# A decoder block's gate/up stage: accumulator X read as a whole, T4 ahead of B22 in the first pair, a ninth place for raw weights, other sums reloaded

## The chip, the cores and the metric

The kernel runs on one core of a Trainium2 chip. The metric is the device time of one execution in microseconds, as the median over several runs. The profile is one execution on the same core; its engines are called PE (TensorE, matmul), DVE (VectorE), ACT (ScalarE), POOL (GpSimd) and SP (SyncE, which here issues most of the DMAs).

## The reference, cut to what matters

The block takes 1024 rows of 1024 numbers in float32. It computes a combined input projection, a causal pooling mixer and a differential attention, merges the two by gates, projects the result, and then runs a feed-forward block. The change touches the feed-forward block alone:

```python
u = rms_norm(h, ffn_pre_g)                                    # (1024, 1024)
f = jax.nn.silu(u @ w_ffn_gate) * (u @ w_ffn_up)              # (1024, 2816)
h = h + rms_norm(f @ w_ffn_down, ffn_post_g)
```

All of it is in float32.

## The kernel before, in words

**Precision.** A float32 product is made of three matmuls in the type fp32r. Each operand is split into a rounded part `hi` (a copy on ACT) and the remainder `lo` (a subtraction on DVE), and `triple` (L2024) adds hi·hi, hi·lo and lo·hi into one accumulator in PSUM.

**Seven products in place of eight.** `u` transposed is cut into four blocks: halves of the contraction by halves of the rows. The weights are cut the same way: halves of the contraction by gate and up. A product of two such 2x2 block matrices is computed with seven block products (Winograd's form of Strassen's method). With g0, g1 the two contraction halves of a block of 128 gate columns and u0, u1 those of the up columns, the weight operands are B11 = g0, B21 = g1, T1 = u0 - g0, T2 = u1 - T1, T3 = u1 - u0, T4 = g1 - T2 and B22 = u1. Their partners are A11, A12, S1, S2, S3, A22 and S4, sums of blocks of `u`. Products are numbered 1 (B11), 2 (B21), 3 (B22), 4 (T4), 5 (T1), 6 (T2) and 7 (T3). Three accumulators take them up:

- Y receives products 1, 6, 7 and 4 in turn. Between two of them its value is copied out by ACT, as the starts of the four results "11", "12", "22" and "21". After product 4, ACT takes the gate's silu straight from Y.
- X receives product 5 and, on top of it, product 3. After product 5 DVE adds X to "22" (in a place named p5); after product 3 it adds X to "12" (in u2).
- Z receives product 2, which DVE adds to "11".

The gated hidden block is silu("11") times "12" for one half of the rows and silu("21") times "22" for the other.

**Units and pairs.** There are 22 blocks of 128 hidden columns. Two blocks, kb and kb + 11, make a group. Group 0 is done ahead of this stage, group 1 as two single units (`unit_products`), and groups 2 to 10 as nine *pairs* (`pair`, L1792). In a pair, each product is done for both blocks, first half "a", then half "b": `P5a` is product 5 of the first block. One such half is 12 matmuls of 128x128 by 128x512. For a pair, X is one tile of two banks, `[128, 2, 512]`, one bank for each block; Y and Z are two tiles each.

**A second level.** From pair 2 on, product 2 of both blocks together is itself done by seven smaller products; from pair 3 on also product 3, and from pair 4 on product 4. Step `3.6` is the sixth inner product of product 3: six matmuls of 128x128 by 128x256 into accumulators Yi, Zi or Xi, each read by an addition on DVE. The sums of blocks that serve as inner operands are formed once on DVE, ahead of their first pair. They don't all fit on chip, and those that the table `STREAM` names are stored to DRAM (`isd`) and loaded again in every pair.

**What sets the order.** The stage isn't written in the order in which it runs. `pair_products` (L1596) states PE's order from the table `STEADY` and hands each operation to a planner (`Plan`), with what it reads and writes, a cost and a due time; a helper's line stands in the profile for all of a kind (L1428 additions and subtractions on DVE, L1432 copies on ACT, L1443 activations, L1446 DMAs). The planner simulates the engines, gives each operation a place (a slot of a pool) when it starts, and emits everything in order of its planned starts. From that order the framework makes the waits between engines, from the tiles that each instruction reads and writes. Raw weights, sums before their split and hidden blocks live in the pool "vf" (eight places of 128x1024 float32, two of which hold the first hidden block and are named F), split operands in the pool "vr" (sixteen).

For PSUM tiles the planner orders a tile's readers and writers on different engines; for a tile of kind "banks" it does so for each bank by itself. In `STEADY`, half `P5a` and half `P5b` of product 5 stand next to each other in pair 2, where `3.x` and `4.x` drop out, and have the steps 3.7, 3.3 and 4.1 between them in later pairs.

The lines that the change touches:

Of the kernel before, what the change touches and what calls it, by code (L numbers as in the profile page):

```python
# [16 lines left out]
P = 128  # L17
# [22 lines left out]

CAPS = {"vr": 16, "vf": 8, "mm": 2, "fil": 2, "pair": 2, "b4": B4, "a8": A8, "wraw": 2, "whi": 2, "wlo": 2, "ft": 2, "sg": 2,
        "small": 20}
BANKS = ("mm", "fil", "pair")
RESERVE = {"E": 2, "gate": 2, "row": 2, "uw": 2}
# [1334 lines left out]

HIDDEN_PATIENCE = {"DVE": 0.05, "ACT": 0.05}
FIRST = {"2": 2, "4": 4, "3": 3}
STREAM = ("2S2", "2S3", "2S4", "3S3", "3S4", "4S2", "4S3")
STASHED, STASH_STEP = range(3, 11), 22
SHARED = ()
OPERANDS = {"2": ("B21", "A12"), "3": ("B22", "S4"), "4": ("T4", "A22")}
# [13 lines left out]
def paired(pl, k, U):  # L1401
# [194 lines left out]
    def pair_products(W, I, T, deep, order, tail, done_with, gated=None):  # L1596


        Y = [bank("mm", "Y") for _ in range(2)]
        X = bank("pair", "X", "banks")  # L1600
        Z = [bank("fil", "Z") for _ in range(2)] if "2" not in deep else None
        acc = {"Y": [(y, None, y) for y in Y], "X": [(X, e, lambda e=e: X()[:, e, :]) for e in range(2)]}
        if Z:
            acc["Z"] = [(z, None, z) for z in Z]
        steps, done = {}, set()
        needs = [{"P1", "P6", "P5", "3.4" if "3" in deep else "P3", "2.4" if "2" in deep else "P2"},
                 {"P7", "P5", "4.4" if "4" in deep else "P4"}]

        def outer(n, e):
            o, w, a = OUTER[n]  # L1610
            s, key, v = acc[o][e]
            product(s, key, v, W[w][e], a, n in "152")
            at = clock[0]

            def to(x):
                t, kt = T[x][e]
                copy(t, v, HALF, [(s, key)], [kt], at + .5)

            def add(x):
                t, kt = T[x][e]  # L1620
                tt(t, v, t, ALU.add, HALF, [(s, key), kt], [kt], at + 2)

            if n == "1":
                to("11")
            if n == "6":
                to("12")
            if n == "7":
                to("22")
                if "4" in deep:
                    to("21")  # L1630
            if n == "5":
                add("22")
                if "3" in deep:
                    add("12")
            if n == "3":
                add("12")
            if n == "2":
                add("11")
            if n == "4":
                gated(e, v, (s, key), at)  # L1640

        def one(x):
            if x[0] == "P":
                outer(x[1], "ab".index(x[2]))
                if x[2] == "b":
                    done.add(x[:2])
            else:
                if x[0] not in steps:
                    steps[x[0]] = inner_steps(W[OPERANDS[x[0]][0]], I[x[0]], T[{"2": "11", "3": "12", "4": "21"}[x[0]]])
                steps[x[0]](x[2])  # L1650
                done.add(x)
            for i in range(2):
                if needs[i] and needs[i] <= done:
                    needs[i] = None
                    done_with(i, clock[0])

        late = {}
        for x in order:
            if x[-1] == "'":
                if x[:-1] in tail:  # L1660
                    tail.pop(x[:-1])()
            elif x[0] != "P" and x[0] not in deep or x[0] == "P" and x[1] in deep:
                continue
            else:
                one(x)
        for x in [x for x in tail]:
            tail.pop(x)()
        if "4" in deep and "4.4" not in order:
            late = {x: (lambda x=x: one(x)) for x in ("4.6", "4.2", "4.7", "4.3", "4.4")}
        return late  # L1670
# [4 lines left out]
def hidden(pl, k):  # L1675
# [116 lines left out]
    def pair(kb, tail):  # L1792
        deep = [x for x in "234" if kb >= FIRST[x]]

        def load(i, kh):
            w = ("w_ffn_gate", "w_ffn_up")[i]
            s = v4(F32, 2, 4, P)
            for e in range(2):
                f = kb + e * FP
                dma(lambda e=e: s()[:, e], lambda f=f: getattr(k, w)[kh * HALF:(kh + 1) * HALF, f * P:(f + 1) * P].rearrange(  # L1800
                    "(k p) n -> p k n", p=P), .26, w=[(s, f"{h + 1}{e + 1}") for h in range(2)])
            return s

        def stashed():
            s = v4(F32, 2, 4, P)
            for e in range(2):
                j, h = divmod(kb - STASHED[0], 2)
                dma(lambda e=e: s()[:, e], lambda e=e: k.tsd[j][:, e, :, h * P:(h + 1) * P], .26,
                    w=[(s, f"{h + 1}{e + 1}") for h in range(2)])
            return s  # L1810

        W = t.pair_weights(load, deep, stashed if kb in STASHED else None)
        q = new_hidden()
        up, p5 = ([temp(s) for _ in range(2)] for s in ("u2", "p5"))
        T = {"11": [q["11"], q["12"]], "21": [q["21"], q["22"]], "12": [(x, x) for x in up], "22": [(x, x) for x in p5]}
        both = set()

        def finish(i, at):
            for e in range(2):
                v, key = q[f"{i + 1}{e + 1}"]  # L1820
                u = (up, p5)[i][e]
                if i == 0 or "4" in deep:
                    silu(v, v, [key], [key], at + 2 + e)
                tt(v, v, u, ALU.mult, HALF, [key, u], [key], at + 3 + e)
            both.add(i)
            if len(both) == 2:
                keep_hidden(kb, q)

        def gated(e, v, key, at):
            o, ko = q[f"2{e + 1}"]  # L1830
            silu(o, v, [key], [ko], at + 1)

        I = {x: t.fetched(x, I2[x]) for x in deep}
        return t.pair_products(W, I, T, deep, STEADY, tail, finish, gated)

    def first_operands():

# [48 lines left out]
def block_kernel(ctx, tc, x, w_in, pool_mix, pool_scale, w_branch_a, lam_q1, lam_k1, lam_q2,  # L1886
# [71 lines left out]
    make_identity(nc, ident)  # L1958
    mhalf = cp.tile([P, 8], F32, name="mhalf")
    nc.vector.memset(mhalf, -0.5)  # L1960
    junk = cp.tile([P, D], mybir.dt.bfloat16, name="junk")
    psc = cp.tile([P, 4], F32, name="psc")
    sgc = cp.tile([P, 1], F32, name="sgc")
    cnt = cp.tile([P, 4, 16], F32, name="cnt")
# [319 lines left out]
    def place(pool, i):  # L2284
        if (pool, i) not in cells:
            if pool == "vr":
                if i < 8:
                    v = W[("B11", "T1", "T2", "B22")[i // 2]][i % 2]().rearrange("p a k n -> p (a k n)")
                else:
                    v = b4([P, D], F32R, "v") if i < B4 else wp.tile([P, D], F32R, tag="wlo", bufs=2, name=name("v"))  # L2290
            elif i < 2:
                v = F[:, i].rearrange("p t c -> p (t c)")
            elif i < 4:
                both = a8([P, 2, D], F32, "v")
                cells["vf", 2], cells["vf", 3] = both[:, 0], both[:, 1]
                v = cells[pool, i]
            else:
                v = wp.tile([P, D], F32, tag=("wraw", "whi", "wlo")[(i - 4) // 2], bufs=2, name=name("v"))
            cells[pool, i] = v
        return cells[pool, i]  # L2300

# [216 lines left out]
```

## Time and profile before

| what | value |
|---|---|
| median of 3 runs | 1237.06 us (1237.05 to 1237.63) |
| the profiled execution's own time | 1236.96 us |
| its span, from the first to the last instruction | 1235.2 us |
| PE busy | 1224.2 us (99% of the span) |
| DVE busy | 965.5 us (78%) |
| ACT busy | 615.1 us (50%) |
| granted TensorE clock, mean | 0.999 |
| gate/up stage | about 647 to 1021 us |

Times in a row of the timeline are the start in us from the span's start, then the duration in us. Behind an instruction the tile it writes stands left of "<-", what it reads to the right; buffer numbers are left out, so that `p` is a place p1 or p5, `u` is u2, and `v`, `Wh`, `Wl`, `F` are places of the pools under the names that they had when they were made. A bracket gives the idle time of the engine just before, and who ended it. Matmuls overlap: one that is recorded as 0.39 us long is followed by the next after less than that, so that the step from start to start is the measure of PE's pace. A row of the table of waits gives the total, the number and the longest of them.

### The profile page before, as it was taken

The page shows a single profiled execution, that of the slowest core. Times are in us where ns is not written, and L with a number is a line of the kernel's source. Part 1 is how long each engine was busy: PE and PEld are TensorE (multiplying, and loading weights), DVE is VectorE, ACT ScalarE, POOL GpSimd, SP SyncE. Part 2 cuts the span into 40 slices and gives each one's busy share as a digit, 9 for nine tenths or more (in the row PEclk, how much of TensorE's full clock was granted, in tenths as well). Part 3 has the DMA queues.
Part 4 walks back from the last instruction along what each step waited for, and adds up shares of the span by engine and source line. Part 5 has one row for each costly group of instructions (what it writes and reads, how often), then busy time and mean ns, then how long its engine had stood idle before and what let it go on. Part 6 is the DMA issues. An engine that isn't in the chain of part 4 may idle for free.

```text
span 1235.2 us, 17203 instructions
## 1 busy us (share of the span) xinstructions
PE 1224.2 (99%) x6292; PEld 1046.7 (85%) x6292; DVE 965.5 (78%) x1628; ACT 615.1 (50%) x1114; POOL 113.4 (9%) x124
## 2 busy tenths in 40 slices
PE   9999999999999999999999999999999999999997
PEld 9888888888899998888888888888888898888886
DVE  6986784634599888885877879998998989965666
ACT  8643444443588773454644433445444455544542
POOL 1000005550201110010000000000000000000223
PEclk9999999999999999999999999999999999999999
DMA  9665248775783027672425555676756599833336
GB/s 372 242 194 188 105 157 268 260 244 183 282 331 137 18 86 256 213 264 80 148 96 172 190 203 159 186 234 210 227 186 198 190 328 320 267 103 94 87 102 213
DMA packets 151573, 240.61 MB, mean 195 GB/s; under 512 B 10688, under 2 KB 85184, under 8 KB 150464
## 3 DMA queue, kind: packets, MB, share of 16 engines
q1 hardware_dynamic: 140896, 203.72, 49.9%
q0 software_dynamic: 4928, 16.78, 4.1%
q10 hardware_dynamic: 5664, 19.01, 3.9%
q8 instruction: 49, 0.80, 0.3%
q14 instruction: 36, 0.29, 0.1%
HBM read 170.01 MB, written 69.47 MB: 194 GB/s over the span
## 4 chain that ended last, share of the span: by engine, by line
PE 94%; DMA 2%; DVE 2%; ACT 1%; issue 0%; SPq 0%; POOLq 0%; DVEq 0%; ACTq 0%
PE Y L2026 9%; PE Y L2027 9%; PE Y L2028 9%; PE X L2026 4%; PE X L2027 4%; PE X L2028 4%; PE Yd L2028 3%; PE Yd L2026 3%; PE Yd L2027 3%; PE s L735 3%; PE o L735 3%; PE qk L567 3%; PE branch L2026 2%; PE branch L2028 2%; PE branch L2027 2%; PE wo L2028 2%
## 5 line engine op out<-in xcount | busy, mean ns | idle before, releaser
L1933 DVE TENSOR_TENSOR w_op<-wd,w_op 128x512 fp32r<-128x512 f32 x72 | 52.2, 725 | 47.5 <-ACT w_op L1981 47.5
L1981 ACT CAST w_op<-wd 128x512 fp32r<-128x512 f32 x72 | 44.8, 623 | 82.6 <-PE Yd L2028 35.5
L2387 POOL TENSOR_TENSOR c<-c,g2post 128x512 f32<-128x512 f32 x12 | 18.3, 1542 | 576.9 <-ACT junk L1974 576.9
L2026 PE MATMUL X<-S_hi,Wh 128*128 128x512 f32 x164 | 64.2, 391 | 0.0
L2027 PE MATMUL X<-S_lo,Wh 128*128 128x512 f32 x164 | 63.9, 390 | 0.0
L2028 PE MATMUL Y<-S_hi,Wl 128*128 128x512 f32 x160 | 62.3, 390 | 0.0
L2026 PE MATMUL Yd<-w_op,s_op 128*128 128x512 f32 x156 | 60.7, 389 | 0.0
L2027 PE MATMUL Yd<-w_op,s_op 128*128 128x512 f32 x156 | 60.7, 389 | 0.0
L2028 PE MATMUL Yd<-w_op,s_op 128*128 128x512 f32 x156 | 60.7, 389 | 0.0
L2026 PE MATMUL Y<-S_hi,Wh 128*128 128x512 f32 x152 | 59.4, 391 | 0.0
L2027 PE MATMUL Y<-S_lo,Wh 128*128 128x512 f32 x152 | 59.3, 390 | 0.0
L2028 PE MATMUL Y<-A_hi,Wl 128*128 128x512 f32 x152 | 59.2, 389 | 0.0
L2028 PE MATMUL X<-S_hi,Wl 128*128 128x512 f32 x148 | 57.6, 389 | 0.0
L925 DVE CUSTOM_DVE_ANT_0 E<-s,negd 128x1024 f32<-128x1024 f32 (+7 forms) x64 | 47.4, 749 | 11.4 <-PE s L735 11.3
L2027 PE MATMUL Y<-A_lo,Wh 128*128 128x512 f32 x144 | 56.2, 390 | 0.0
L2026 PE MATMUL Y<-A_hi,Wh 128*128 128x512 f32 x144 | 56.2, 390 | 0.0
L1933 DVE TENSOR_TENSOR s_op<-s_raw,s_op 128x512 fp32r<-128x512 f32 x69 | 52.8, 766 | 1.2 <-ACT s_op L1981 1.2
L931 ACT ACTIVATE E<-E,nm 128x1024 f32<-128x1024 f32 (+7 forms) x64 | 49.6, 776 | 6.9 <-DVE nm L925 6.7
L1432 ACT CAST v<-v 128x1024 fp32r<-128x1024 f32 (+2 forms) x46 | 38.9, 858 | 28.3 <-DVE v L1428 9.5
L1933 DVE TENSOR_TENSOR Wl<-wf_t,Wh 128x1024 fp32r<-128x1024 f32 x34 | 45.7, 1359 | 6.4 <-ACT Wh L1995 3.4
L2026 PE MATMUL wo<-woh,mh 128*128 128x512 f32 x128 | 50.5, 394 | 0.0
L2028 PE MATMUL wo<-woh,ml 128*128 128x512 f32 x128 | 49.9, 390 | 0.0
(638 smaller groups left out, 3936.6 us busy)
## 6 DMA issues: line engine op xcount, KB each, us to landing
v<-isd SPq DMA_DIRECT2D x31, 512.0 KB, 4.1
s_raw<-fsd SPq DMA_DIRECT2D x31, 512.0 KB, 3.7
fsd<-v SPq DMA_DIRECT2D x53, 256.0 KB, 3.5
w_raw<-in_w_in_dram SPq DMA_DIRECT2D x24, 512.0 KB, 5.0
wd<-in_w_ffn_down_dram SPq DMA_DIRECT2D x44, 256.0 KB, 5.5
Wl<-isd SPq DMA_DIRECT2D x17, 512.0 KB, 3.7
sgs<-sgd SPq DMA_DIRECT2D x16, 512.0 KB, 9.5
sgd<-g_st ACTq DMA_DIRECT2D x14, 512.0 KB, 6.2
```

The costliest lines, as they stand in the source:

```text
L567: nc.tensor.matmul(o()[:, cs], l, r, start=first and kk == 2 * kh and j == 0, stop=last and kk == 2 * kh + 1 and j == len(todo) - 1, skip_ ...
L735: nc.tensor.matmul(o, l, r, start=start, stop=stop, skip_group_check=skip)
L925: V.tensor_tensor_reduce(out=view[m]().rearrange("p (j w) -> p j w", j=nj), in0=sc()[:, :nj, :w], in1=negd()[:, S - L:S].rearrange("p (j w ...
L931: A.activation(view[m](), view[m](), AF.Exp, bias=nm()[:, m:m + 1], scale=-1.0, accum_out=sums()[:, m:m + 1])
L1432: return pl.op("ACT", act(n), lambda: A.copy(o(), a()), r=r, w=w, rank=rank, claim=claim)
L1933: nc.vector.tensor_tensor(out=o, in0=a, in1=f32(hi), op=ALU.subtract)
L1981: nc.scalar.copy(hi, a)
L2026: nc.tensor.matmul(o, ah, bh, start=start, stop=False, skip_group_check=goes_on)
L2027: nc.tensor.matmul(o, ah, bl, start=False, stop=False, skip_group_check=goes_on)
L2028: nc.tensor.matmul(o, al, bh, start=False, stop=stop, skip_group_check=goes_on)
L2387: eng.tensor_tensor(out=where, in0=src, in1=g2post[:, c], op=ALU.mult)
```

## The change

Five things differ.

- X in a pair is now a plain tile for the planner, so that its two banks are no longer ordered apart. The reads of X that follow a product (the new `taken`) are recorded only after the second half of that product, for both halves in a row. For Y and Z nothing changes.
- In pair 2, where products 3 and 4 are both outer ones, the order ends with P4a, P3a, P4b, P3b in place of P3a, P3b, P4a, P4b.
- Pool "vf" has nine places. The ninth is a tile `extra` of 128x1024 float32, allocated for the whole kernel, whose first half also serves as the scratch `junk` into which the sums of squares write their unused output.
- Product 3 reloads its sums S2 and S4 (before: S3 and S4), product 4 its S2 and S4 (before: S2 and S3).
- From these the planner makes another order on DVE, ACT and SP and other places for the tiles.

```diff
-CAPS = {"vr": 16, "vf": 8, "mm": 2, "fil": 2, "pair": 2, ...
+CAPS = {"vr": 16, "vf": 9, "mm": 2, "fil": 2, "pair": 2, ...
...
-STREAM = ("2S2", "2S3", "2S4", "3S3", "3S4", "4S2", "4S3")
+STREAM = ("2S2", "2S3", "2S4", "3S2", "3S4", "4S2", "4S4")
...
-        X = bank("pair", "X", "banks")
+        X = bank("pair", "X")
...
             product(s, key, v, W[w][e], a, n in "152")
+            if o != "X":
+                taken(n, e)
+            elif e == 1:
+                taken(n, 0)
+                taken(n, 1)
+
+        def taken(n, e):
+            s, key, v = acc[OUTER[n][0]][e]
             at = clock[0]
...
-        return t.pair_products(W, I, T, deep, STEADY, tail, finish, gated)
+        order = STEADY if "3" in deep else STEADY[:-4] + ("P4a", "P3a", "P4b", "P3b")
+        return t.pair_products(W, I, T, deep, order, tail, finish, gated)
...
-    junk = cp.tile([P, D], mybir.dt.bfloat16, name="junk")
+    extra = cp.tile([P, D], F32, name="extra")
+    junk = extra.bitcast(mybir.dt.bfloat16)[:, :D]
...
-                v = wp.tile([P, D], F32, tag=("wraw", "whi", "wlo")[(i - 4) // 2], bufs=2, name=name("v"))
+                v = extra if i == 8 else wp.tile([P, D], F32, tag=("wraw", "whi", "wlo")[(i - 4) // 2], bufs=2, name=name("v"))
```

Three places where the order moved. The first is on DVE, in the second unit, around the additions of Z to p1 and of Y to p5, while PE runs that unit's products T3, B22 and T4. (In these rows the names are cut as in `p_1155`, which is a place p5.) Before:

```order
L1428 TENSOR_TENSOR Wl_5983<-v_6136,Wl_5983 128x512
L1428 TENSOR_TENSOR p_1152_6250<-Z_6280,p_1152_6250 128x512
L1428 TENSOR_TENSOR A_lo_5252<-v_6136,A_hi_5243 128x2x256
L1428 TENSOR_TENSOR v_6136<-v_6133,v_6080 128x1024
L1428 TENSOR_TENSOR v_6080<-F_5809,v_6136 128x1024
L1428 TENSOR_TENSOR Wh_6020<-v_6136,Wl_6019 128x1024
L1428 TENSOR_TENSOR p_1155_6278<-Y_6213,p_1155_6278 128x512
```

Now:

```order
L1428 TENSOR_TENSOR Wl_5983<-v_6133,Wl_5983 128x512
L1428 TENSOR_TENSOR v_6080<-v_6080,extra 128x1024
L1428 TENSOR_TENSOR extra<-F_5809,v_6080 128x1024
L1428 TENSOR_TENSOR p_1152_6252<-Z_6282,p_1152_6252 128x512
L1428 TENSOR_TENSOR Wh_6020<-v_6080,Wl_6019 128x1024
L1428 TENSOR_TENSOR p_1155_6280<-Y_6213,p_1155_6280 128x512
```

The two differences of pair 2's weights (T1 and T2 before their split) went ahead of the Z addition, and the split of A12's inner sum went behind; one 1024-wide instruction is left between the two additions. Sums of A12 that stood in F before are in other places, and F takes u1 in their stead.

The second is on PE and DVE, in pair 2, behind the last matmuls of product 5 (operands S1 and T1). PE before:

```order
L2027 MATMUL X_6540<-S_lo_5739,Wl_6019 128x512
L2028 MATMUL X_6540<-S_hi_5724,Wh_6020 128x512
L2026 MATMUL X_6540<-S_hi_5876,v_6270 128x512
L2027 MATMUL X_6540<-S_lo_5912,v_6270 128x512
L2028 MATMUL X_6540<-S_hi_5876,Wh_6002 128x512
```

PE now (the line numbers are ten higher):

```order
L2037 MATMUL X_6539<-S_lo_5739,Wl_6019 128x512
L2038 MATMUL X_6539<-S_hi_5724,Wh_6020 128x512
L2036 MATMUL Y_6359<-A_hi_5713,v_6272 128x512
L2037 MATMUL Y_6359<-A_lo_5726,v_6272 128x512
L2038 MATMUL Y_6359<-A_hi_5713,Wh_6002 128x512
```

DVE before:

```order
L1428 TENSOR_TENSOR v_6080<-v_6136,v_6080 128x1024
L1428 TENSOR_TENSOR p_1166_6509<-X_6540,p_1166_6509 128x512
L1428 TENSOR_TENSOR F_5809<-F_5809 128x256 x2
L1428 TENSOR_TENSOR p_1168_6556<-X_6540,p_1168_6556 128x512
L1428 TENSOR_TENSOR v_6161<-F_5809,Wh_6020 128x1024
```

DVE now:

```order
L1428 TENSOR_TENSOR v_6114<-v_6080,Wh_5984 128x256
L1428 TENSOR_TENSOR p_1166_6508<-X_6539,p_1166_6508 128x512
L1428 TENSOR_TENSOR p_1168_6552<-X_6539,p_1168_6552 128x512
L1428 TENSOR_TENSOR F_5809<-F_5809,extra 128x1024
L1428 TENSOR_TENSOR v_6230<-S_hi_5876,S_lo_5912 128x512 x2
```

Product 3 (S4, A side) came right behind product 5 on X; now a half of product 4 on Y comes between, and the two reads of X follow each other.

The third is on DVE in pair 3, around the reads of X after product 5. Before:

```order
L1428 TENSOR_TENSOR v_6208<-v_6133,v_6230 128x1024
L1428 TENSOR_TENSOR v_6080<-v_6230,v_6080 128x1024
L1428 TENSOR_TENSOR p_1176_6800<-X_6863,p_1176_6800 128x512
L1428 TENSOR_TENSOR u_1173_6728<-X_6863,u_1173_6728 128x512
L1428 TENSOR_TENSOR u_1175_6765<-u_1175_6765,Yi_6810 128x256
L1428 TENSOR_TENSOR Wl_5983<-v_6133,Wl_5950 128x512
L1428 TENSOR_TENSOR u_1175_6765<-u_1175_6765,Xi_6837 128x256
L1428 TENSOR_TENSOR v_6133<-v_6133 128x256
L1428 TENSOR_TENSOR Wl_5983<-v_6133,Wl_5950 128x256
```

Now:

```order
L1428 TENSOR_TENSOR v_6133<-v_6230,v_6133 128x1024
L1428 TENSOR_TENSOR p_1176_6797<-X_6862,p_1176_6797 128x512
L1428 TENSOR_TENSOR u_1173_6717<-X_6862,u_1173_6717 128x512
L1428 TENSOR_TENSOR p_1179_6851<-X_6862,p_1179_6851 128x512
L1428 TENSOR_TENSOR u_1173_6717<-u_1173_6717,Yi_6810 128x256
L1428 TENSOR_TENSOR u_1175_6760<-X_6862,u_1175_6760 128x512
```

The two reads of the second half (p_1179 and the second u) stood eight rows further down before; now all four reads of X stand together, with one addition of Yi among them, and the splits that stood between them come earlier or later.

2 lines of the change are left out of this document (1 added, 1 removed).

## The prediction

> **What bounds the kernel now.** I read the page's busy times first, then the waits of PE, then PE's timeline at each wait, and last DVE's timeline beside it.
>
> ```profile
> PE 1224.2 (99%) x6292; PEld 1046.7 (85%) x6292; DVE 965.5 (78%) x1628; ACT 615.1 (50%) x1114; POOL 113.4 (9%) x124
> ```
>
> PE is busy for 1224.2 of 1235.2 us, so nothing beside PE's own idle time can be won. The profiled execution took 1236.96 us, 1.76 us of it outside the span, and lies 0.10 us under the median of 1237.06. The waits of PE in the whole run:
>
> ```profile
> PE X L2026 <- DVE p L1428: 1.6, 2, 0.9
> PE warm L343 <- POOL ident masks.py:199: 1.4, 1, 1.4
> PE qk L567 <- ACT A_hi L483: 1.0, 2, 0.5
> PE X L2026 <- DVE u L1428: 0.3, 1, 0.3
> PE Y L2026 <- DVE p L1428: 0.2, 1, 0.2
> ```
>
> The second and third lie in the opening, which the change leaves alone. The other three all name L1428, the helper that records VectorE operations, and so lie in the gate/up stage or just ahead of it. The stretch of that stage, 647.0 to 1021.4:
>
> ```profile
> 647.00:1021.40 374.40, 372.23 (x2107) 326.58 (x2106) 330.79 (x576) 164.61 (x251) 0.00 (x0) 1.00 0.65 208
> ```
>
> PE is idle for 374.40 - 372.23 = 2.17 us there, at a granted clock of 1.00, and DVE is busy for 88%. "Idle" understates what a wait costs, because matmuls overlap. So I take starts. PE at the four waits:
>
> ```profile
> 678.45 0.39 PE L2028 MATMUL X<-S_hi,Wl 128*128 128x512 f32 x1
> 679.04 0.50 PE L2026 MATMUL Y<-A_hi,v 128*128 128x512 f32 x1 [0.20 <-DVE p L1428]
> 679.37 0.39 PE L2027 MATMUL Y<-A_lo,v 128*128 128x512 f32 x1
> ...
> 708.56 0.39 PE L2028 MATMUL X<-S_hi,Wh 128*128 128x512 f32 x1
> 709.73 0.50 PE L2026 MATMUL X<-S_hi,v 128*128 128x512 f32 x1 [0.79 <-DVE p L1428]
> 710.07 0.39 PE L2027 MATMUL X<-S_lo,v 128*128 128x512 f32 x1
> ...
> 712.13 0.39 PE L2027 MATMUL X<-S_lo,v 128*128 128x512 f32 x1
> 712.36 0.39 PE L2028 MATMUL X<-S_hi,Wh 128*128 128x512 f32 x1
> 713.60 0.50 PE L2026 MATMUL X<-S_hi,v 128*128 128x512 f32 x1 [0.85 <-DVE p L1428]
> 713.94 0.40 PE L2027 MATMUL X<-S_lo,v 128*128 128x512 f32 x1
> ...
> 749.66 0.28 PE L2026 MATMUL Xi<-v,Wl 128*128 128x256 f32 x1
> ...
> 750.26 0.28 PE L2028 MATMUL Xi<-v,Wh 128*128 128x256 f32 x1
> 750.87 0.50 PE L2026 MATMUL X<-S_hi,v 128*128 128x512 f32 x1 [0.32 <-DVE u L1428]
> 751.21 0.40 PE L2027 MATMUL X<-S_lo,v 128*128 128x512 f32 x1
> ```
>
> Undisturbed, a 512-wide matmul follows the one before after 0.23 us (712.13 to 712.36) and a 256-wide one after 0.12 (749.66 to 750.26 are five steps). The matmul behind a waiting one comes after 0.33 or 0.34, so each restart costs 0.11 more. The losses:
>
> - W1, second unit, T4 product: 0.59 - 0.23 + 0.11 = 0.47
> - W2, first pair (pair 2), first half of B22 (P3a): 1.17 - 0.23 + 0.11 = 1.05
> - W3, first pair, second half (P3b): 1.24 - 0.23 + 0.11 = 1.12
> - W4, second pair (pair 3), second half of T1 (P5b): 0.61 - 0.12 + 0.11 = 0.60
>
> Together 3.24 us, all that the stage has to give. After 751 PE waits for nothing up to the stage's end.
>
> **The change part by part.** The amount of work stays the same on every engine; what moves is order and place.
>
> *W2 and W3: T4 ahead of B22, X read whole.* DVE in the first pair:
>
> ```profile
> 708.99 0.69 DVE L1428 TENSOR_TENSOR p<-X,p 128x512 f32<-128x512 f32 x1 [1.66 <-PE X L2028]
> ...
> 712.86 0.69 DVE L1428 TENSOR_TENSOR p<-X,p 128x512 f32<-128x512 f32 x1 [2.38 <-PE X L2028]
> ```
>
> Both additions found DVE idle, and each began 0.04 to 0.11 us after a product on X ended: the first after the second half of T1 (708.56 + 0.39), although it reads the first half, which was done 2.7 us sooner; the second after P3a (712.36 + 0.39), although its half was done at 708.95. So waits here go by the whole accumulator, and P3b waited for an addition that itself waited for P3a. In the new order the two additions stand together behind T1: 708.99, and 0.60 later (the step of 749.53 to 750.13, below) 709.59, done at 710.28. PE meanwhile writes the first T4 half into Y, twelve matmuls of 0.227, from 708.79 to 711.51. P3a then finds X read 1.2 us ago, and P3b follows another T4 half. W2 and W3 are gone: 2.17 us. T4 now starts 7.7 us sooner; its last operand must be ready by 708.8. The nearest row is the last 1024-wide split of that group:
>
> ```profile
> 693.61 1.22 DVE L1428 TENSOR_TENSOR Wh<-v,v 128x1024 fp32r<-128x1024 f32 x1
> ```
>
> It ends 14 us before that, and the new DVE order has both splits at the same depth. If this cover were gone the price would be a new wait of at most W2's size. What is late next: P3b ends 3.2 us later against the pair's other work, so the additions of B22 and the hidden products of this pair come later; PE's next pair doesn't read them. I take the full 2.17 (bounds 1.05 and 2.17).
>
> *W1: the ninth place.* DVE ahead of W1:
>
> ```profile
> 673.43 0.69 DVE L1428 TENSOR_TENSOR p<-Z,p 128x512 f32<-128x512 f32 x1 [1.56 <-PE Z L2028]
> ...
> 674.76 1.23 DVE L1428 TENSOR_TENSOR v<-v,v 128x1024 f32<-128x1024 f32 x1
> 676.02 1.23 DVE L1428 TENSOR_TENSOR v<-F,v 128x1024 f32<-128x1024 f32 x1
> 677.16 1.22 DVE L1428 TENSOR_TENSOR Wh<-v,Wl 128x1024 fp32r<-128x1024 f32 x1
> 678.29 0.69 DVE L1428 TENSOR_TENSOR p<-Y,p 128x512 f32<-128x512 f32 x1
> ```
>
> PE waits for the last row. It stands 4.86 us behind the Z addition, three 1024-wide instructions between, and ahead of that DVE had nothing for 1.56 us. With the sums of A12 out of F, the two differences move ahead of the Z addition: 1.26 + 1.14 = 2.40 us, of which 1.56 fall into the idle time. The Z addition begins 0.84 late at 674.27, one split (1.13) follows 0.60 later, and the Y addition is free to start at 676.0; Y's own product is done twelve matmuls before 678.68, about 676.1. So the addition ends by 676.9, 1.8 ahead of PE. The weights must be there by 671.8:
>
> ```profile
> 664.08 1.20 SPq L1446 DMA_DIRECT2D F<-in_w_ffn_up_dram  x2
> ```
>
> The same load stands at the same place in SP's queue and has 7 us. I take the full 0.47 (bounds 0 and 0.47).
>
> *W4: X read after both halves.* The chain that ended last before W4, and DVE there:
>
> ```profile
> 731.25 5.47 DMA fsd<-F
> 736.78 5.89 DMA F<-in_w_ffn_up_dram
> ...
> 749.53 0.68 DVE L1428 TENSOR_TENSOR p<-X,p 128x512 f32<-128x512 f32 x1
> 750.13 0.68 DVE L1428 TENSOR_TENSOR u<-X,u 128x512 f32<-128x512 f32 x1
> ```
>
> The second half of T1 waits for two reads of the first half, which came late because DVE was late, after a weight load that had to wait until hidden values had left its place. With all four reads behind P5b nothing on DVE stands before P5b: 0.60 gained (bounds 0 and 0.60).
>
> [...]
>
> *Later pairs.* There the early reads cost nothing, and late ones could:
>
> ```profile
> 787.77 0.68 DVE L1428 TENSOR_TENSOR u<-X,u 128x512 f32<-128x512 f32 x1
> 789.11 0.40 PE L2026 MATMUL X<-S_hi,v 128*128 128x512 f32 x1
> 809.46 0.41 DVE L1428 TENSOR_TENSOR v<-v,Yi 128x256 f32<-128x256 f32 x1
> 810.73 0.28 PE L2026 MATMUL Yi<-v,Wl 128*128 128x256 f32 x1
> ```
>
> The read ends at 788.45, 0.66 ahead of P5b: no gain. Two additions (2 x 0.60) move behind P5b, and the tightest read that PE needs afterwards ends at 809.87, 0.86 ahead. It comes over 15 us after P5b, with DVE idle 12% of the time between, so I take 0 (bounds: 0, and the loss of the third rival).
>
> *Reloaded sums.* As many are stored and reloaded as before. Product 3 uses S2 three small steps and one large product ahead of S4 (3 x 0.72 + 2.72 = 4.9 us).
>
> ```profile
> 735.56 0.42 SPq L1446 DMA_DIRECT2D v<-isd  x1
> v<-isd SPq DMA_DIRECT2D x31, 512.0 KB, 4.1
> ```
>
> S4's reload, issued at 735.56 and 4.1 us long, feeds the matmul at 749.66: 10 us of cover, 5 left for S2. Cost 0; if the cover failed, at most the reload's 4.1 once. *Scratch inside the new place*: the squares that write it run before the stage or long after; 0.
>
> Sum: 2.17 + 0.47 + 0.60 = 3.24. 1236.96 - 3.24 = 1233.72, and with the 0.10 to the median **1233.8 us** (0.26% faster).
>
> **Rivals.**
>
> *The load chain holds (no change).* W4 hangs on the DMA chain of 731 to 742, not on PE. PE now arrives 0.47 + 2.17 = 2.64 us sooner; if the chain stays at its hour, DVE stays late, and another accumulation of the second pair (a Yi read behind the same 1024-wide work) takes W4's place, for up to 2.64 us. For it: two 5 us transfers in the chain. Against: in the new order this load goes to another place than F, and P5b no longer waits. Half of it is 1.3: 1235.1; all of it: 1236.5.
>
> *The change does nothing.* If PE waited at W2 to W4 for DVE's place in its queue rather than for the reads of X, it would wait as long as before: 1237.0. Against it: both additions of the first pair found DVE idle.
>
> *Slower: late reads in the later pairs.* Two additions, 1.20 us, land behind each P5b, at worst with the other two, 2.40. Once DVE is over 0.86 late at the Yi read, PE stops: 2.40 - 0.86 + 0.11 = 1.65 in each of seven pairs, 11.6 us less the 3.24: 1245.4. With 1.20 it is 0.45 x 7 = 3.2, about 1237. [...]
>
> **How the numbers follow.** Forecast 0.72, chain 0.20, nothing 0.04, slower 0.04. A measurement tells about 0.2%, 2.5 us, from no change: below 1234.6. The forecast falls there, with a margin of 0.8, and a small chain loss too; so faster 0.73, same 0.23, slower 0.04. The range runs from 1233.0 (all four waits and 0.7 of spread, as the shown runs have 0.6) to 1236.4 (the chain rival almost whole).
>
> **What would show it.** PE's waits on L1428 gone in the changed profile; four reads of X in one run behind P5b; X additions in the first pair 0.6 us apart; the Y addition before 677. Wrong would be: a PE wait on Yi between 715 and 760 (chain), or one of the same size every 37 us from 790 on (late reads).

## The result, and the profile after

The changed kernel takes 1233.64 us, the median of 9 runs, against 1237.06 us before on the same chip: a ratio of 0.9972 with a 95% interval from 0.9962 to 0.9983, or 3.4 us. One of the nine runs took 3548 us, at a granted clock of 1.00 and for a reason that nothing on record shows; the ratio is of the other eight, which lie between 1232.95 and 1234.80 with a median of 1233.47. The forecast was 1233.8. The profiled execution took 1233.3 us with a span of 1231.5, which is 3.7 us less than before in both.

The first part of the page after, and PE's waits in the whole run:

```profile
PE 1222.8 (99%) x6292; PEld 1046.9 (85%) x6292; DVE 962.6 (78%) x1628; ACT 614.7 (50%) x1114; POOL 113.5 (9%) x124
```

```profile
PE warm L343 <- POOL ident masks.py:199: 1.4, 1, 1.4
PE qk L567 <- ACT A_hi L483: 1.1, 2, 0.6
```

The number of instructions is the same on every engine. What is left of PE's waits is the two of the opening; the three lines that named L1428 are gone. The gate/up stage as one stretch (its length, then the busy time and the number of instructions on PE, weight loads, DVE, ACT and POOL, the granted clock, the DMA share and GB/s):

```profile
646.87:1017.90 371.03, 371.03 (x2104) 326.58 (x2103) 328.10 (x574) 165.05 (x250) 0.00 (x0) 1.00 0.66 211
```

PE was idle for 2.17 us there before, and is idle for none now. DVE does as much as before and is still 88% busy, so it is the order of its work that changed, not its load.

**Where the time went.** To weigh the stage without the opening, whose length differs from run to run, I take PE's starts from one matmul that both kernels have at the same place, the first on Z behind 606 us, to the last matmul of the run. Before, and after:

```profile
607.03 0.39 PE L2026 MATMUL Z<-A_hi,Wh 128*128 128x512 f32 x1
...
1228.40 0.39 PE L2028 MATMUL Yd<-w_op,s_op 128*128 128x512 f32 x1
```

```profile
606.90 0.39 PE L2036 MATMUL Z<-A_hi,Wh 128*128 128x512 f32 x1
...
1224.96 0.39 PE L2038 MATMUL Yd<-w_op,s_op 128*128 128x512 f32 x1
```

621.37 us before, 618.06 after: 3.31 us gained between the two. The four waits W1 to W4 made 3.24. Of the whole 3.66, 0.13 lies ahead of the first row, where the order of work is the same, and about 0.2 behind the last matmul. PE's timeline after, at W1's place, in the first pair (P4a, P3a, and P3b further on), and at W4's place:

```profile
678.32 0.39 PE L2038 MATMUL X<-S_hi,Wl 128*128 128x512 f32 x1
678.55 0.39 PE L2036 MATMUL Y<-A_hi,v 128*128 128x512 f32 x1
...
707.92 0.39 PE L2038 MATMUL X<-S_hi,Wh 128*128 128x512 f32 x1
708.15 0.39 PE L2036 MATMUL Y<-A_hi,v 128*128 128x512 f32 x1
...
710.64 0.39 PE L2038 MATMUL Y<-A_hi,Wh 128*128 128x512 f32 x1
710.87 0.39 PE L2036 MATMUL X<-S_hi,v 128*128 128x512 f32 x1
...
716.08 0.39 PE L2038 MATMUL Y<-A_hi,Wh 128*128 128x512 f32 x1
716.31 0.39 PE L2036 MATMUL X<-S_hi,v 128*128 128x512 f32 x1
...
747.40 0.28 PE L2038 MATMUL Xi<-v,Wl 128*128 128x256 f32 x1
747.52 0.40 PE L2036 MATMUL X<-S_hi,v 128*128 128x512 f32 x1
```

T4's first matmul (678.55), P3a (710.87), P3b (716.31) and P5b (747.52) stood behind a wait before; now every second row of two follows its first at the undisturbed step, 0.23 and at the last place 0.12. DVE after, at W1 and then at the first pair's X:

```profile
671.66 1.22 DVE L1428 TENSOR_TENSOR v<-v,extra 128x1024 f32<-128x1024 f32 x1
672.91 1.23 DVE L1428 TENSOR_TENSOR extra<-F,v 128x1024 f32<-128x1024 f32 x1
674.06 0.68 DVE L1428 TENSOR_TENSOR p<-Z,p 128x512 f32<-128x512 f32 x1
...
676.03 0.69 DVE L1428 TENSOR_TENSOR p<-Y,p 128x512 f32<-128x512 f32 x1 [0.15 <-PE Y L2038]
...
708.35 1.29 DVE L1428 TENSOR_TENSOR p<-X,p 128x512 f32<-128x512 f32 x2 [5.67 <-PE X L2038]
```

The two differences went ahead of the Z addition, and the Y addition ends at 676.72, 1.8 us before PE needs it. The two X additions stand in one run, and end at 709.64, 1.23 ahead of P3a.

### The profile page after: what moved, and what is told of

Read it like the earlier page. It is cut to its first block, busy times and chain, and to the rows that moved or that the text cites. A ratio compares the mean times of both kernels' runs of the same rounds, so it can differ in the third digit from the quotient of the medians.

```text
span 1231.5 us, 17212 instructions
## 1 busy us (share of the span) xinstructions
PE 1222.8 (99%) x6292; PEld 1046.9 (85%) x6292; DVE 962.6 (78%) x1628; ACT 614.7 (50%) x1114; POOL 113.5 (9%) x124
## 4 chain that ended last, share of the span: by engine, by line
PE 97%; DMA 1%; ACT 1%; SPq 0%; issue 0%; DVE 0%; POOLq 0%; DVEq 0%; ACTq 0%
PE Y L2036 10%; PE Y L2037 9%; PE Y L2038 9%; PE X L2036 4%; PE X L2037 4%; PE X L2038 4%; PE Yd L2037 3%; PE Yd L2036 3%; PE Yd L2038 3%; PE s L735 3%; PE o L735 3%; PE qk L567 3%; PE branch L2036 2%; PE branch L2038 2%; PE branch L2037 2%; PE wo L2038 2%
## 5 line engine op out<-in xcount | busy, mean ns | idle before, releaser
L2038 PE MATMUL Y<-S_hi,Wl 128*128 128x512 f32 x168 | 65.5, 390 | 0.0
L2038 PE MATMUL Y<-A_hi,Wl 128*128 128x512 f32 x168 | 65.4, 389 | 0.0
L2036 PE MATMUL Y<-S_hi,Wh 128*128 128x512 f32 x160 | 62.5, 391 | 0.0
L2037 PE MATMUL Y<-S_lo,Wh 128*128 128x512 f32 x160 | 62.5, 390 | 0.0
L2036 PE MATMUL X<-S_hi,Wh 128*128 128x512 f32 x156 | 61.0, 391 | 0.0
L2037 PE MATMUL X<-S_lo,Wh 128*128 128x512 f32 x156 | 60.7, 389 | 0.0
L2036 PE MATMUL Y<-A_hi,Wh 128*128 128x512 f32 x152 | 59.3, 390 | 0.0
L2037 PE MATMUL Y<-A_lo,Wh 128*128 128x512 f32 x152 | 59.3, 390 | 0.0
L925 DVE CUSTOM_DVE_ANT_0 E<-s,negd 128x1024 f32<-128x1024 f32 (+7 forms) x64 | 47.3, 747 | 11.4 <-PE s L735 11.3
L1991 ACT CAST s_op<-s_raw 128x512 fp32r<-128x512 f32 x69 | 42.6, 617 | 25.7 <-DMA s_raw<-fsd 25.1
L2038 PE MATMUL X<-S_hi,Wl 128*128 128x512 f32 x140 | 54.5, 389 | 0.0
```

What stands on the lines that cost most here:

```text
L925: V.tensor_tensor_reduce(out=view[m]().rearrange("p (j w) -> p j w", j=nj), in0=sc()[:, :nj, :w], in1=negd()[:, S - L:S].rearrange("p (j w ...
L1991: nc.scalar.copy(hi, a)
L2036: nc.tensor.matmul(o, ah, bh, start=start, stop=False, skip_group_check=goes_on)
L2037: nc.tensor.matmul(o, ah, bl, start=False, stop=False, skip_group_check=goes_on)
L2038: nc.tensor.matmul(o, al, bh, start=False, stop=stop, skip_group_check=goes_on)
```

## The experiments

The working names: W1 is the wait in the second unit, W2 and W3 those at P3a and P3b in the first pair (pair 2), W4 that at P5b in pair 3. In this table "stage" is the stretch from the first matmul on Z to the last matmul, as above, as its difference to before's 621.37; "gain" is the difference of the medians to the runs of the kernel before on the same chip. The last column is the cost of each PE wait from 640 us on by starts: what its matmul and the one behind it come later than an undisturbed step.

| kernel | median, us (runs) | gain | stage | PE's losses behind 640 us |
|---|---|---|---|---|
| changed kernel | 1233.64 (9) | 3.42 | -3.31 | none |
| X alone | 1235.53 (10) | 1.54 | -0.46 | W1 0.47, P3a 1.65, Yi 0.59, Xi 0.10 |
| order alone | 1235.29 (10) | 1.78 | -1.36 | W1 0.48, Y 0.81, W4 0.59 |
| ninth place alone | 1236.51 (10) | 0.56 | -0.56 | W2 1.05, W3 1.13, W4 0.47 |
| reloaded sums alone | 1236.73 (10) | 0.34 | +0.22 | W1 0.47, W2 1.05, W3 1.12, W4 0.22, five of 0.11 |
| all but X | 1235.08 (10) | 2.12 | -1.67 | P5b: 0.27, 0.51, five of 0.18 |
| all but the order | 1234.90 (10) | 2.30 | -1.64 | P3a 1.65 |
| all but the ninth place | 1233.86 (6) | 3.34 | -2.71 | W1 0.47, Y 0.11 |
| all but the reloaded sums | 1233.62 (6) | 3.58 | -3.31 | none |
| X and order | 1235.46 (10) | 1.60 | -1.64 | W1 0.47, Y 1.19 |
| X of pair 2 as two tiles | 1234.35 (10) | 2.71 | -2.36 | W1 0.47, W4 0.48 |
| changed, two late instructions | 1234.83 (10) | 2.23 | -1.77 | 0.91, four of 0.16 |
| changed, four late instructions | 1245.80 (4) | -8.74 | +8.04 | 3.38, four of 1.61, 1.55 of halved clock |

The losses, less the 3.24 of the kernel before, give the stage column within 0.12. The medians agree with it within 0.7 us except for "X alone", which is 1.1 us faster than its stage says. The opening has the same order of work in all of these kernels, and the first matmul on Z started at 606.5 to 607.7 in all profiles but one (608.5, four late instructions); 0.51 of the 1.1 lies there in that kernel's profile, 0.23 behind its last matmul, and 0.34 between the profiled executions of the two kernels and their medians. One profile for each kernel doesn't tell what of this belongs to the kernel and what to the run, so I rest no verdict below a microsecond on a median, and read the parts from PE's starts, which repeat: the start of W1's matmul is 0.36 late in all six of these kernels that still have it. For the place alone and the reloaded sums alone, the 95% intervals of the ratio (0.9988 to 1.0007 and 0.9990 to 1.0008) include no change. The medians of X alone, of all but the order and of the two tiles lie 0.4 to 0.6 below the times that were expected.

### X alone

```diff
-        X = bank("pair", "X", "banks")
+        X = bank("pair", "X")
...
+            if o != "X":
+                taken(n, e)
+            elif e == 1:
+                taken(n, 0)
+                taken(n, 1)
```

> The kernel before, with X alone changed: a plain tile, its reads recorded behind the second half of a product. Theory (waits go by the whole X tile; each of W1 to W4 has its own cause): W4 (0.60 us at 750.87) goes. In the first pair T4 still stands behind B22, so P3a comes right behind P5b and has to wait for both additions of X, which run one after the other: start to start 708.56 to about 710.3, a loss of about 1.65 in place of W2's 1.05. W3 (1.12) goes, since the second addition stands right behind the first. W1 (0.47) stays. Waits of 2.1 in all, a gain of about 1.1, less if a Yi in a later pair is met late by some tenths: 1236.0 to 1236.4. Load-chain rival: the 0.60 of W4 comes back as a PE wait on Yi between 750 and 760, so a gain of 0.5 at most. Rival of late reads: a PE wait on Yi or X every 37 us from 790 on, 0.45 or more each, and the time above 1237. Rival of DVE's place (the change does nothing): W2, W3 and W4 as before, 1237.0.

PE at the first half of B22, and later at a Yi between pairs 4 and 5:

```profile
708.04 0.39 PE L2036 MATMUL X<-S_hi,Wh 128*128 128x512 f32 x1
709.81 0.50 PE L2034 MATMUL X<-S_hi,v 128*128 128x512 f32 x1 [1.38 <-DVE p L1428]
...
798.33 0.39 PE L2036 MATMUL Y<-A_hi,Wh 128*128 128x512 f32 x1
799.05 0.39 PE L2034 MATMUL Yi<-v,v 128*128 128x256 f32 x1 [0.33 <-DVE v L1428]
```

W3 and W4 are gone, W1 stays, and P3a loses 1.65 to both additions, all as the theory had it. The load-chain rival wanted a wait between 750 and 760; there is none. The late reads do strike, but once: 0.59 at the first Yi behind pair 4 and 0.10 at an Xi behind that, and nothing every 37 us. In the stage, X alone brings 0.46 of the 3.31.

### The order alone

```diff
+        order = STEADY if "3" in deep else STEADY[:-4] + ("P4a", "P3a", "P4b", "P3b")
+        return t.pair_products(W, I, T, deep, order, tail, finish, gated)
```

> The kernel before, with the order P4a P3a P4b P3b in the first pair alone; X still read half by half. Theory: W2 and W3 (1.05 and 1.12) go, since a product on Y lies between T1 and each half of B22. W1 (0.47) stays, W4 (0.60) stays within 0.3. Y's second product of the second pair may now meet an ACT copy late (its due times move), by up to 0.8 near 726. Gain 1.2 to 2.2: 1234.9 to 1235.9. Rival of DVE's place: W2 and W3 don't shrink, since the additions stand in the same row of DVE's order: 1237.0. Load-chain rival: W4 grows by what W2 and W3 gave, to about 2.7, and the time is 1237.0.

PE in pair 3, at Y's second product:

```profile
725.48 0.28 PE L2029 MATMUL Yi<-A_hi,v 128*128 128x256 f32 x1
726.30 0.50 PE L2027 MATMUL Y<-S_hi,v 128*128 128x512 f32 x1 [0.54 <-ACT v L1432]
```

W2 and W3 are gone, with X still read half by half; 0.81 comes back at a copy of Y on ACT. W4 stays at 0.59, where the load-chain rival said 2.7. So the order alone removes W2 and W3, and 2.17 - 0.81 = 1.36 is left of their worth.

### The ninth place alone, and the reloaded sums alone

```diff
-CAPS = {"vr": 16, "vf": 8, "mm": 2, ...
+CAPS = {"vr": 16, "vf": 9, "mm": 2, ...
...
-    junk = cp.tile([P, D], mybir.dt.bfloat16, name="junk")
+    extra = cp.tile([P, D], F32, name="extra")
+    junk = extra.bitcast(mybir.dt.bfloat16)[:, :D]
...
```

> The kernel before, with the ninth place for raw weights alone (and the scratch laid into it). Theory: W1 alone goes, 0.47; W2, W3 and W4 stay at 1.05, 1.12 and 0.60 within 0.1: 1236.6. Load-chain rival: the weight load no longer waits for F in the second pair, so W4 shrinks or goes too: 1236.0. If the place does nothing by itself: 1237.0, with the Y addition still at about 678.3.

```diff
-STREAM = ("2S2", "2S3", "2S4", "3S3", "3S4", "4S2", "4S3")
+STREAM = ("2S2", "2S3", "2S4", "3S2", "3S4", "4S2", "4S4")
```

> The kernel before, with the other choice of reloaded sums alone. Prediction: cost 0, so 1237.0, with the same four waits. Against it: reading the orders of both kernels anew, with half-by-half reads of X and eight places DVE's order in the later pairs has one more instruction ahead of the last read of X between P5a and P5b. By that reading W4 shrinks to about 0.3, but P5b waits 0.17, a loss of 0.28 with the restart, in each of six or seven later pairs: 1238.0, with PE waits on X every 37 us from 823 on.

The place removes W1 and 0.12 of W4, 0.56 in the stage. DVE in that kernel has the Y addition where the theory put it, waiting only for Y's own product:

```profile
676.79 0.69 DVE L1428 TENSOR_TENSOR p<-Y,p 128x512 f32<-128x512 f32 x1 [0.16 <-PE Y L2029]
```

The reloads alone shrink W4 to 0.22 and cost 0.11 in each of five later pairs; the stage is 0.22 longer: nearer to the prediction's 0 than to the 1.0 that I had read from the orders in between. The five have the form shown under the hardware below.

### All but X

```diff
-        X = bank("pair", "X")
+        X = bank("pair", "X", "banks")
...
-            if o != "X":
-                taken(n, e)
-            elif e == 1:
-                taken(n, 0)
-                taken(n, 1)
```

> The changed kernel, with X again of kind "banks" and read half by half; the order, the ninth place and the reloaded sums stay changed. By the prediction's sum this gives back W4 alone, 0.60: 1234.2. By the orders read anew it gives back much more: with nine places and the new reloads, P5b meets the early reads of X late not once but in each of the pairs 3 to 9, by 0.3 to 0.7 each with the restart, 3 us in all: 1236.7, with PE waits on X every 37 us from 747 on. Load-chain rival: one wait between 745 and 760, none later.

DVE and PE at P5b of pair 4:

```profile
785.72 0.68 DVE L1428 TENSOR_TENSOR p<-X,p 128x512 f32<-128x512 f32 x1
786.32 0.68 DVE L1428 TENSOR_TENSOR u<-X,u 128x512 f32<-128x512 f32 x1
```

```profile
786.53 0.28 PE L2030 MATMUL Yi<-A_hi,v 128*128 128x256 f32 x1
787.06 0.50 PE L2028 MATMUL X<-S_hi,Wh 128*128 128x512 f32 x1 [0.24 <-DVE u L1428]
```

The second early read ends at 787.00, and P5b starts 0.06 behind it. In the kernel before the same read ended 0.66 ahead of P5b. With the other parts of the change DVE reaches these reads later, and the early reads cost something in each of seven pairs: 0.27 + 0.51 + 5 x 0.18 = 1.68. So reading X whole is worth 1.64 us within this change, and 0.46 by itself. Neither the sum (0.60) nor my later reading (3) had the size.

### All but the order, the place, the reloaded sums

```diff
-        order = STEADY if "3" in deep else STEADY[:-4] + ("P4a", "P3a", "P4b", "P3b")
-        return t.pair_products(W, I, T, deep, order, tail, finish, gated)
+        return t.pair_products(W, I, T, deep, STEADY, tail, finish, gated)
```

> The changed kernel, with B22 ahead of T4 in the first pair again. Theory: one PE wait only, at P3a of the first pair, for both additions of X: about 1.65 (0.60 above W2's 1.05, since the second addition comes on top); no W3. 1233.6 + 1.65 = 1235.3. If waits went by X's halves, P3a would wait for nothing it doesn't now, and the time would stay at 1233.6. If whole reading did nothing for P3b, there would be two waits, 2.2 in all: 1235.8.

```diff
-CAPS = {"vr": 16, "vf": 9, "mm": 2, ...
+CAPS = {"vr": 16, "vf": 8, "mm": 2, ...
...
-    extra = cp.tile([P, D], F32, name="extra")
-    junk = extra.bitcast(mybir.dt.bfloat16)[:, :D]
+    junk = cp.tile([P, D], mybir.dt.bfloat16, name="junk")
...
```

> The changed kernel, with eight places for raw weights and the scratch by itself. Theory: W1 alone comes back, 0.47 at about 679, nothing else: 1234.1. Load-chain rival: with F back as the place of the second pair's load, PE waits on a Yi or X between 735 and 760 too, for up to 2.6: 1235 to 1236.7.

```diff
-STREAM = ("2S2", "2S3", "2S4", "3S2", "3S4", "4S2", "4S4")
+STREAM = ("2S2", "2S3", "2S4", "3S3", "3S4", "4S2", "4S3")
```

> The changed kernel, with the sums reloaded as before. Prediction: the choice costs and brings nothing, no PE wait in the stage: 1233.6, within 0.3. Rival: the choice is what makes the ninth place reach W1 (sums of A12 and the first reloads share SP's queue there), and W1's 0.47 comes back: 1234.1.

Without the order and without the place, PE's waits are those that were foreseen. Without the order P3a starts 1.77 us behind the matmul ahead of it (707.55 and 709.32), as with X alone: 1.77 - 0.23 + 0.11 = 1.65. It is W1's 0.47 without the place (with another 0.11 at 725). Without the place F again takes a weight load of pair 3, and PE waits nowhere between 735 and 760. Without the new reloads the stage is the same as in the changed kernel to 0.01 us.

### X and the order together

Both diffs above, on the kernel before.

> The kernel before, with X read whole and the new order in the first pair, but eight places and the old reloads. Prediction's sum: W2, W3 and W4 go, 2.17 + 0.60; W1 stays: 1237.06 - 2.77 = 1234.3. By the orders read anew this is too good: without the ninth place the second pair's copies of Y on ACT stand behind weight splits that come late, and PE waits about 1.2 for a copy near 726 and 0.4 near 797: 1235.9. Load-chain rival: the same wait, but on Yi, with the load of F ahead of it.

ACT, then PE, at Y's second product in pair 3:

```profile
724.62 0.62 ACT L1432 CAST Wh<-v 128x512 fp32r<-128x512 f32 x1 [5.00 <-DVE v L1428]
...
726.70 1.06 ACT L1432 COPY v<-Y 128x512 f32<-128x512 f32 x2
```

```profile
726.12 0.28 PE L2037 MATMUL Yi<-A_hi,v 128*128 128x256 f32 x1
727.32 0.50 PE L2035 MATMUL Y<-S_hi,v 128*128 128x512 f32 x1 [0.93 <-ACT v L1432]
```

The copies of Y stand on ACT behind three casts whose source DVE delivers late, and PE waits 1.19 for them. The expected second wait near 797 isn't there. With the reloads added ("all but the ninth place") 1.08 of this goes; with the place added ("all but the reloaded sums") all of it. So the prediction's sum of independent parts would have been 1.1 too high for this half of the change.

### X of the first pair as two tiles

```diff
-        X = bank("pair", "X", "banks")
+        X = [bank("pair", "X") for _ in range(2)] if "3" not in deep else bank("pair", "X", "banks")
...
+            acc["X"] = [(x, None, lambda x=x: x()[:, 0, :]) for x in X]
```

> The kernel before, unchanged in the order of every engine, but with X of the first pair as two tiles (one for each block, each in its own slot) in place of one tile with two banks. Only the waits between engines can differ. Theory (waits go by the whole tile): the first addition now starts when P5a ends, about 706.2 rather than 708.99, and P3a finds it done; the second starts at about 709.0 and is over before P3b; W2 and W3 go, 2.17, while W1 and W4 stay: 1234.9. Rival of DVE's place in its queue: the additions start where they did, W2 and W3 stay: 1237.0. Between the two (a wait for the neighbouring half lies on PE's side alone): W3 goes, W2 stays, 1235.9.

All engines run the same instructions in the same order as in the kernel before. DVE, and PE:

```profile
705.79 1.22 DVE L1428 TENSOR_TENSOR v<-v,v 128x1024 f32<-128x1024 f32 x1
706.93 0.69 DVE L1428 TENSOR_TENSOR p<-X,p 128x512 f32<-128x512 f32 x1
...
708.74 0.69 DVE L1428 TENSOR_TENSOR p<-X,p 128x512 f32<-128x512 f32 x1 [0.33 <-PE X L2032]
```

```profile
708.24 0.39 PE L2032 MATMUL X<-S_hi,Wh 128*128 128x512 f32 x1
708.47 0.39 PE L2030 MATMUL X<-S_hi,v 128*128 128x512 f32 x1
```

The first addition starts at 706.93, as soon as DVE is done with what stands ahead, in the middle of P5b; before, it stood idle for 1.66 us at the same place and began when P5b had ended. P3a follows P5b after 0.23. W2 and W3 are gone with nothing but the tiles changed: the waits went by the whole tile. The chain rival falls here too. SP issues the weight load into F at 733.49, and at 736.03 in the kernel before. PE stands 2.54 us earlier there, 2.17 of it from W2 and W3, and the load has come 2.54 sooner with it: the chain follows PE, and W4 shrinks, from 0.60 to 0.48.

DVE's addition of 706.93 to 707.62 reads one of the two tiles while PE writes the other, with no wait on either side: the matmuls from 706.88 to 707.56 start 0.22 to 0.23 apart. So the waits of the first pair came from the tile that both blocks shared; with a tile for each, the chip did both at once. W4, at 750.87 in the kernel before, lies in pair 3, where X stayed one tile in this run: that it has the same cause is likely, but not shown.

### The price of late reads

```diff
                 if "3" in deep:
                     add("12")
+                    LATE.append(e)
+                    for _ in range(2 * e if len(LATE) % 16 in range(1, 13) else 0):
+                        x, kx = T["12"][1]
+                        pl.op("DVE", .001, lambda x=x: V.tensor_tensor(out=x(), in0=x(), in1=x(), op=ALU.max), ...
```

The condition picks pairs 3 to 8.

> The changed kernel, with two more 512-wide instructions on DVE (the maximum of u2 with itself, which leaves its value) right behind the reads of X after P5b, in six pairs (3 to 8). This prices the third rival: how late DVE may be before PE stops. By the prediction's cover of 0.86 at the tightest Yi read and 0.60 for each addition: (1.20 - 0.86) + 0.11 = 0.45 in each of six pairs, 2.7 us: 1236.3, PE waits on Yi every 37 us. If DVE's idle time (12%) takes them up: 1233.6, no wait. If they cost in full: 6 x 1.31 = 7.9: 1241.5.

The second has `4 * e` in place of `2 * e`.

> As with two, but four more instructions, 2.40 us, in each of the six pairs. By the cover: (2.40 - 0.86) + 0.11 = 1.65 in each of six pairs, 9.9 us: 1243.5, of which 7.2 over the run with two. If DVE's idle time takes them up: below 1236. If they cost in full: 6 x 2.51 = 15.1: 1248.7.

PE with two, and with four, at the first Yi behind pair 5:

```profile
834.45 0.39 PE L2043 MATMUL Y<-A_hi,Wl 128*128 128x512 f32 x1
834.73 0.39 PE L2041 MATMUL Yi<-Wh,v 128*128 128x256 f32 x1
```

```profile
840.10 0.39 PE L2043 MATMUL Y<-A_hi,Wl 128*128 128x512 f32 x1
841.84 0.39 PE L2041 MATMUL Yi<-Wh,v 128*128 128x256 f32 x1 [1.35 <-DVE v L1429]
```

The read of Yi that this matmul waits for, with its matmul, in the changed kernel; then the read with two, and with four (the helper's line is one higher there):

```profile
832.27 0.41 DVE L1428 TENSOR_TENSOR v<-v,Yi 128x256 f32<-128x256 f32 x1
...
833.81 0.28 PE L2036 MATMUL Yi<-Wh,v 128*128 128x256 f32 x1
```

```profile
834.26 0.42 DVE L1429 TENSOR_TENSOR v<-v,Yi 128x256 f32<-128x256 f32 x1
```

```profile
841.36 0.42 DVE L1429 TENSOR_TENSOR v<-v,Yi 128x256 f32<-128x256 f32 x1
```

Pair 3 cost PE nothing in either. Behind pair 4 they cost 0.91 with two (the profile has ACT's write of F end that wait, after 0.67 us of idle time) and 3.38 with four, and in each of pairs 5 to 8 0.16 and 1.61, where the cover of 0.86 gave 0.45 and 1.65. The near hit with four is luck. The 0.86 had been read at another Yi; here the read ends at 832.68 in the changed kernel, so that the cover is 1.13. With two it ends at 834.68, just when the matmul is due (834.45 + 0.23): all of the cover is used up, and little more than a restart is lost. With four it ends 1.45 behind the hour at which the matmul is due (840.10 + 0.23), so DVE is 1.13 + 1.45 = 2.58 late and not 2.40. With four, more cover and more lateness than was reckoned nearly cancel; with two the lateness is 1.13 against a reckoned 1.20, and nothing makes up for the larger cover. Behind pair 4 the cover is less, 0.73: in the changed kernel the read ends at 796.04 and the matmul starts at 796.77.

So the rival's mechanism exists, but the place and the cover in its price were not the ones that count. What it lacked in this change is the lateness. Up to the cover lateness cost next to nothing (behind pair 5, 0.16 for 1.13 us of it), and beyond it PE stopped for about as long as DVE was late (with four, the read ended 1.45 behind the hour and the matmul started 1.51 behind it). By PE's starts two instructions cost 1.55 in all, where 2.7 was expected, and four cost 11.4 with the clock (the last section), where 9.9 was expected.

## Why the prediction was right

**The bound, and the four waits.** Right. PE's idle time was all there was, and the 3.24 read from starts came back as 3.31 in the stage. All signs named beforehand appeared: no PE wait on L1428, X additions 0.6 us apart in the first pair, the Y addition done at 676.72 (forecast 676.9), P3a 1.2 us behind the reads of X (forecast 1.2, measured 1.23). One sign holds with a blemish: in pairs 3 to 9 the four reads of X behind P5b have an addition of a Yi between the third and the fourth, and in the last pair more stands between them.

**W2 and W3, by the order and by the whole tile.** Shown. The order alone removes both, the two tiles alone remove both, and X alone turns them into the 1.65 that follows from two additions on end. The prediction gave both to order and X together; for these two waits the order is enough.

**W1, by the ninth place.** Shown from both sides: the place alone removes it, and without the place it returns at 0.47.

**W4, by reading X whole.** Right that it goes so, and mis-sized as the worth of that part. The step that failed is the sentence on the later pairs, "There the early reads cost nothing": true of the kernel before, where they had 0.66 to spare in pair 4, but the other parts of the change use this up, and early reads would then cost 1.68 in seven pairs. Reading X whole was worth 1.64 in this change, 0.46 alone. The total came out right because X was read whole in the same change.

**Reloaded sums at 0.** Right beside the other three parts (0.00). Not right as a general price: alone they cost 0.22, and where X and the order are changed but the place isn't, they are worth 1.08. What they moved there isn't the reload's cover, on which the prediction argued, but the hour at which ACT comes to a copy of Y: in the rows above it stood behind a cast that waited 5.00 us for DVE. The prediction didn't look at this; that nothing of it is left beside the other three parts is luck. For the scratch inside the ninth place, also put at 0, nothing speaks against it: at the earliest the first matmul on Z started at 606.5 with the scratch there and at 606.5 with the scratch by itself.

**Adding the parts.** The four parts alone bring 0.46 + 1.36 + 0.56 - 0.22 = 2.16 of 3.31; taken out one at a time they cost 1.64, 1.67, 0.60 and 0.00. The sum over the four waits held, since it was made over places where the changed kernel was known from its order to wait no more. A sum over the parts of the change wouldn't have held.

**The rivals.** The load chain is refuted: with the old load into F and PE 2.54 earlier, the load came 2.54 earlier and W4 didn't grow. "Does nothing" is refuted by the two tiles. The late reads are real but weren't reached. Two readings in their price were off: DVE was idle for 8% and not 12% of the stretch that was meant (busy for 18.81 of 20.40 us from 789.1 to 809.5 in the kernel before), and the cover that gives way first is not the 0.86 at 810.73 but, in the changed kernel, the 0.73 at the first Yi behind pair 4.

**What stays open.** Some tenths of a microsecond between the medians and the stage, and the reason of the whole 1.1 us for X alone. The opening's length varied by about a microsecond between profiles with the same order of work in it (606.5 to 607.7 at the first matmul on Z, but for one), which would be enough for the tenths and for half of the 1.1, but one profile for each kernel doesn't show that it is the cause. That W4 too comes from the shared tile and not from the chip is inferred from the first pair.

## What to carry to other kernels

When an engine waits for a reader of an accumulator, look at whether the reader itself found its engine idle, as the additions behind W2 and W3 did (for 1.66 and 2.38 us). Here it was the granularity of the wait that cost, and either splitting the tile or putting a product on another accumulator between removed both waits, 2.17 us. Cost such a change over the waits of the new order, place by place, not over the parts of the edit: here one part was worth 0.46 alone and 1.64 among the others. And where the bound engine has no more idle time, measure how much lateness its tightest covers still take (0.73 us here) before moving more work behind them.

## What the runs showed of the hardware

**A restart cost 0.11 us even where the wait itself cost nothing.** With the reloads alone, PE at P5b of pair 5:

```profile
825.59 0.28 PE L2028 MATMUL Yi<-A_hi,Wh 128*128 128x256 f32 x1
825.70 0.49 PE L2026 MATMUL X<-S_hi,Wl 128*128 128x512 f32 x1
826.03 0.39 PE L2027 MATMUL X<-S_lo,Wl 128*128 128x512 f32 x1
```

The first matmul on X starts on its step of 0.11 to 0.12, and the one behind it still comes after 0.33 in place of 0.23. The read of X ended at 825.65 there, 0.05 ahead. The table of waits has no line for these: they are seen by starts alone, five times 0.11.

**Behind an idle time of 3.15 us the granted clock fell to half.** With four late instructions, the wait behind pair 4, and windows from its end on (columns as above; the clock is the third number from the right):

```profile
798.12 0.39 PE L2043 MATMUL Y<-A_hi,Wh 128*128 128x512 f32 x1
801.66 0.36 PE L2041 MATMUL Yi<-Wh,v 128*128 128x256 f32 x1 [3.15 <-DVE v L1429]
```

```profile
801.70:804.70 3.00, 3.00 (x18) 3.00 (x19) 2.37 (x5) 1.30 (x2) 0.00 (x0) 0.67 0.47 135
804.70:806.00 1.30, 1.30 (x5) 1.07 (x4) 0.98 (x2) 0.28 (x1) 0.00 (x0) 0.50 1.03 278
806.20:812.00 5.80, 5.80 (x36) 5.10 (x35) 3.58 (x7) 2.98 (x5) 0.00 (x0) 1.00 0.93 310
...
841.90:846.00 4.10, 4.10 (x27) 3.77 (x28) 3.59 (x7) 1.58 (x2) 0.00 (x0) 1.00 0.37 106
```

A mean of 0.67 over the first 3.0 us is 1.0 us at full clock and 2.0 at half, and PE's starts agree: it went on at full pace for a microsecond after its restart (256-wide matmuls 0.12 apart up to 802.68), then at about half of it (0.21 apart, and 0.42 to 0.43 in place of 0.23 for the 512-wide ones) until about 806.1, and lost another 1.55 us by starts. Behind the first of the four waits with 1.35 us of idle time the clock was 1.00 (the last row). The long wait, 3.15 us idle and 3.54 from start to start, was a single one; it cost 3.38 by itself, and PE lost about half as much again at the lower clock behind it. One such wait doesn't show that the idle time is what brought the clock down.
